# A planner that counts DMA time: order of the first loads, four key projections side by side, and sums of squares on GpSimd

## The chip, the cores and the metric

The kernel runs on one core of one Trainium2 chip. The metric is the device time of one launch in microseconds (us): lower is better. A core has a matrix engine (PE, with its weight loads shown as PEld), a vector engine (DVE), an activation engine (ACT), GpSimd (POOL) and a queue engine that issues the DMAs (SP). Each engine works through its own instructions in the order in which they stand in the program. An instruction that has to wait for a semaphore holds up everything behind it on its engine.

## The reference, cut to what matters

Two transformer-like blocks run one after the other on x of 512 tokens by 2048 features. All arithmetic is 32-bit. The change touches mainly the beginning of the first block:

```python
mem_n = rms_norm(mem, mem_norm_g)               # mem: 256 x 2048
h = rms_norm(x, norm_g[i])                      # x: 512 x 2048
proj = jnp.einsum("bsd,de->bse", h, dn_w_in[j])
kv = jnp.einsum("bmd,de->bme", mem_n, w_kv)     # 1024 columns of k, 1024 of v
k = rms_norm(kv[..., :XA_WIDTH].reshape(B, -1, XA_HEADS, XA_DIM), kn_g)
v = kv[..., XA_WIDTH:].reshape(B, -1, XA_HEADS, XA_DIM)
# ... gated delta rule on proj, cross attention on k and v, gate, w_out,
# then a second block (mLSTM, HGRN2, w_out_2, a gated feed of p)
```

## The kernel before, in words

**Tiling.** Tensors lie with features on the 128 partitions. x is 16 tiles `xraw` of 128x512 (256 KB each), mem is 8 tiles `mraw`, each of which holds two feature tiles of 128x256 (256 KB each). A projection is a `Job`: 128 output columns, accumulated over 16 feature tiles in one PSUM bank. Its weights arrive in four *pieces* `raw` of four feature tiles (256 KB each). To keep 32-bit accuracy, every operand is split into two parts: `hi`, a rounded copy made by ACT, and `lo`, the rest, made by DVE (`lo = raw - hi`). Each feature tile takes three matmuls: hi by hi, hi by lo, lo by hi. So one piece is 12 matmuls, and each piece costs one ACT and one DVE instruction of 128x512 ahead of it.

**The order.** The program's order is written once, when the kernel is built, by the class `Driver`. It keeps a modelled clock for each engine (`clk`, line 87). Every helper (`act`, `tt`, `stt`, `mm`) emits an instruction and moves the clock of its engine (`_on`, line 105). A task (a Python generator) runs on when its own time `tau` is no later than the modelled PE clock; `run` (line 348) picks the task with the lowest priority number that may run, and otherwise the next unit of a projection (`_unit`, line 315). A time that is modelled too early puts an instruction into its engine's queue too early, where it then blocks. `calm` (line 222) holds back background work while the clocks of ACT or DVE are too far ahead of PE's.

**DMAs.** All of them are issued by SP. `_pump` (line 266) loads the pieces, at most six buffers `raw` at a time, and takes for the landing of piece i the later of PE's clock plus 3.0 us and 4.5 + 1.5 i us. `d.dma` (line 171), used for everything that is stored and loaded later on, adds 2.3 us. Neither knows of other transfers under way.

**The beginning.** `first_loads` (line 447) adds one load behind each of the first 24 pieces: `mraw` 1 to 7 behind the first seven, then `ident`, `norm_g` and `xraw` 0, then one `xraw` behind each piece. The key projections 0 and 1 run side by side (their pieces alternate), all others one by one. `mem_task` (line 560) splits mem's tiles, then sums mem's squares; the sum passes through PE (`col_sum`) and ACT, and the result `f_rm` is what every key and value evacuation (`evac_k`, `evac_v`) waits for. `x_task` (line 591) makes the square of each `xraw` on ACT (`xsq`) and adds it to `xsum` on DVE. When the sum is done, sixteen `part` tasks scale each tile (DVE), copy it to `xh` (ACT) and take the rest `xl` (DVE). The first projection of x (`w_xq`) comes behind the last value projection. In `x_task` the load's time `f_x[k].tau` is read by `need`, but nothing yields between that and the emission of `xsq`.

Of the kernel before, what the change touches and what calls it, by code (L numbers as in the profile page):

```python
# [16 lines left out]
MUL, ADD, SUB, MAX = ALU.mult, ALU.add, ALU.subtract, ALU.max  # L17

T = 512
NM = 256  # L20
C = 128
NCH = T // C
# [56 lines left out]
class Driver:  # L79
# [4 lines left out]

    def __init__(self, tc, wp, psp, sp):
        self.tc, self.nc, self.wp, self.psp, self.sp = tc, tc.nc, wp, psp, sp
        self.clk = dict(pe=0.0, act=0.0, dve=0.0, pool=0.0)
        self.tau = 0.0
        self.tasks = []
        self.units = []  # L90
        self.pieces = []
        self.i_unit = self.i_dma = self.i_hi = self.i_spl = self.i_mm = 0
        self.spl_end = []
        self.nbank, self.nacc, self.maxacc = 0, 0, 6
        self.bank_t = [0.0] * 8
        self.bank_of = {}
        self.live = 0
        self._dep, self._last = 0.0, None
        self.held = {}
        self.nslot = 0  # L100
        self.table = None
        self.nhead, self.head = 0, None
# [65 lines left out]
                              is_transpose=True if tr else None)  # L168
        self._on("pe", c, LP)

    def dma(self, out, in_, lat=2.3):
        self.nc.sync.dma_start(out=out, in_=in_)
        self.tau = max(self.tau, self.clk["pe"]) + lat


    def slot(self, shape=(128, T), dt=F32, name="s", reserve=0):
# [89 lines left out]
    def _pump(self):  # L266
        while self.i_dma < len(self.pieces):
            r = self.i_dma - RAW
            if r >= 0 and (r >= self.i_spl or self.spl_end[r][1] > self.clk["pe"]):
                break  # L270
            j, c0, n = self.pieces[self.i_dma]
            raw = self.wp.tile([128, KC, 128], F32, tag="raw", bufs=RAW, name="raw")
            self.nc.sync.dma_start(out=raw[:, :n, :j.w.shape[2]], in_=j.w[:, c0:c0 + n])
            self.pieces[self.i_dma] = (j, c0, n, raw, max(self.clk["pe"] + 3.0, 4.5 + 1.5 * self.i_dma))
            self.i_dma += 1
            if self.i_dma <= self.nhead:
                self.head(self.i_dma)
        while self.i_hi < self.i_dma and self.i_hi < self.i_mm + SPL:
            j, c0, n, raw, tau = self.pieces[self.i_hi]
            if tau > self.clk["pe"] and self.i_hi > self.i_mm:  # L280
                break
            hi = self.wp.tile([128, KC, 128], F32R, tag="hi", bufs=SPL, name="hi")
            self.tau = tau
            m = j.w.shape[2]
            self.act(hi[:, :n, :m], raw[:, :n, :m], AF.Copy)
            self.pieces[self.i_hi] = (j, c0, n, raw, hi, self.tau)
            self.i_hi += 1
        while self.i_spl < self.i_hi:
            j, c0, n, raw, hi, tau = self.pieces[self.i_spl]
            if tau > max(self.clk["pe"], self.clk["dve"]) and self.i_spl > self.i_mm:  # L290
                break
            self.tau = tau
            if j.narrow:
                lo = None
                self.tt(hi[:, :n, 64:], raw[:, :n, :64], hi[:, :n, :64], SUB)
            else:
                lo = self.wp.tile([128, KC, 128], F32R, tag="lo", bufs=SPL, name="lo")
                self.tt(lo[:, :n], raw[:, :n], hi[:, :n], SUB)
            self.pieces[self.i_spl] = (j, c0, n, hi, lo, self.tau)
            self.spl_end.append((self.i_spl, self.tau))  # L300
            self.i_spl += 1
# [94 lines left out]
def build(ctx: ExitStack, tc: tile.TileContext, A, out):  # L396
# [47 lines left out]
    for k in range(KT):  # L444
        xraw.append(d.slot_now(name="xraw"))

    def first_loads(i):

        if i < len(mraw):
            nc.sync.dma_start(out=mraw[i], in_=A["memT"][:, 2 * i:2 * i + 2])  # L450
        elif i < len(mraw) + KT:
            k = i - len(mraw)
            if k == 0:
                nc.sync.dma_start(out=ident, in_=A["ident"])
                nc.sync.dma_start(out=norm_g, in_=A["norm_g"])
            nc.sync.dma_start(out=xraw[k], in_=A["xT"][:, k])
            d.give(f_x[k])
            f_x[k].tau = d.clk["pe"] + 3.0

    f_x = [Fut() for _ in range(KT)]  # L460
    resetb = const.tile([128, T], F32, name="resetb")
    nc.vector.memset(resetb, 1.0)
# [97 lines left out]
    def mem_task():  # L560
        hs = []
        for i, t in enumerate(mraw):
            d.tau = 3.8 + 1.5 * i
            yield
            tau = d.tau
            hi = yield from slot(dt=F32R, name="mh")
            lo = yield from slot(dt=F32R, name="ml")
            hi = hi.rearrange("p (k m) -> p k m", k=2)
            lo = lo.rearrange("p (k m) -> p k m", k=2)
            for j in range(2):  # L570
                g = mem_norm_g[:, 2 * i + j:2 * i + j + 1]
                d.tau = tau
                act(hi[:, j], t[:, j], AF.Copy, scale=g)
                stt(lo[:, j], t[:, j], g, hi[:, j], MUL, SUB)
                give(M.f[2 * i + j], (hi[:, j], lo[:, j]))
        ssum = None
        t0 = d.tau
        for i, t in enumerate(mraw):
            d.tau = t0
            yield from d.calm(AHEAD)  # L580
            t = t.rearrange("p k m -> p (k m)")
            act(t, t, AF.Square)
            if i == 0:
                ssum = t
            else:
                tt(ssum, ssum, t, ADD)
                free(t)
        tt(ssum[:, :NM], ssum[:, :NM], ssum[:, NM:], ADD)
        yield from ones_sum([ssum[:, :NM]], NM, 1.0 / D, f_rm)

    def x_task():
        ssum = yield from slot(name="xsum")
        for k, t in enumerate(xraw):
            yield from need(f_x[k])
            yield from d.calm(AHEAD)
            q = yield from slot(name="xsq")
            act(q, t, AF.Square)
            if k == 0:
                cp(ssum, q)
            else:  # L600
                tt(ssum, ssum, q, ADD)
            free(q)
        f = Fut()
        yield from ones_sum([ssum], T, 1.0 / D, f)
# [134 lines left out]
    def evac_ab(job):  # L739
# [19 lines left out]
               rows[0:32, (n + 1) * C - 1:(n + 1) * C], SUB, -1.0, MUL)  # L759
        dgc = tc.dram_tile([32, T], F32, name="dgc")  # L760
        yield
        d.dma(dgc, rows[0:32])
        pt = yield from transpose4(rows)
        for nm in ("gb", "ngc", "beta", "kdec", "nbeg"):
            gate[nm] = const.tile([128, NCH, 32], F32, name=nm)
# [497 lines left out]
    def evac_if(job):  # L1263
# [33 lines left out]
        dws = tc.dram_tile([32, NCH], F32, name="dws")  # L1297
        yield
        for j, r in enumerate((mu, wi, en)):
            d.dma(drow[j], r[0:32], lat=0)  # L1300
        d.dma(dws, ws[:, 0:NCH])
        t0 = d.tau
        pt = yield from transpose4(rows)
        wc = const.tile([128, NCH, 64], F32, name="wc")
# [2 lines left out]
        wsb = const.tile([128, 32, NCH], F32, name="wsb")  # L1307
        d.tau = t0
        yield
        d.dma(wsb, bc(dws, 0, 128))  # L1310
        free(w, fx, nb, mu, wi, en, rows, sp_)
        mlg.update(drow=drow, wc=wc, wsb=wsb)
        give(f_if)
# [26 lines left out]
    def ml_task(h):  # L1340
# [4 lines left out]
        for j in range(3):  # L1345
            t = yield from slot(name="rowb")
            yield
            d.dma(t, mlg["drow"][j, h:h + 1].broadcast_to((128, T)))
            rr.append(t)
        muR, qd, enR = rr  # L1350
        yield
# [381 lines left out]

    first_loads(0)
    d.head = first_loads
    d.nhead = len(mraw) + KT
    d.spawn(mem_task(), 1)
    d.spawn(x_task(), 2)
    jk = [Job(A["w_k"][e], M, evac_k(e), NM) for e in range(2 * XH)]
    jv = [Job(A["w_v"][e], M, evac_v(e), NM) for e in range(2 * XH)]  # L1740
    d.add(jk[0], jk[1])
    for j in jk[2:] + jv[:-2]:
        d.add(j)
    jv[-1].drop = True
    d.add(jv[-2], jv[-1])
# [241 lines left out]
```

## Time and profile before

| what | us |
|---|---|
| median of 3 runs | 2911.86 (2909.01 to 2912.65) |
| the profiled execution | 2909.73 |
| its span, first to last instruction | 2907.8 |
| PE busy in the span | 2852.8 (98%) |
| DVE busy, ACT busy, POOL busy | 1713.4, 1389.0, 80.7 |
| DMA, mean over the span | 106 GB/s |

The profiled execution lies 2.13 us below the median of the runs. PE is busy for nearly the whole span. What is left to it are its idle gaps, and stretches in which its matmuls are slower than elsewhere. The views by stretch show in which part of the run these lie, and the timeline shows which instruction of which engine each of them ended with.

### The profile page before, as it was taken

To read this page: it belongs to the slowest core of one execution; us is meant where nothing else is said; L and a number is where in the kernel's file an instruction comes from. 1 tells how busy PE (TensorE), PEld (TensorE's weight loads), DVE (VectorE), ACT (ScalarE), POOL (GpSimd) and SP (SyncE) were. 2 spreads that over 40 slices of the span, in tenths; PEclk is the share of its full clock that TensorE was granted. 3 is DMA by queue.
4 is the path that set the end of the run, shared out by engine and by line. 5 is a ranking of instruction groups with operands and counts; after the bars stand their busy time and mean duration, and the time that the engine had idled before them with its cause. 6 is when DMAs were issued, how large, how long until landed. Compare 5 with 4: busy or idle time off the path is not lost. (4 is left out here: it accounts for less than half of the span.)

```text
span 2907.8 us, 40891 instructions
## 1 busy us (share of the span) xinstructions
PE 2852.8 (98%) x14936; PEld 2382.5 (82%) x14936; DVE 1713.4 (59%) x3285; ACT 1389.0 (48%) x2627; POOL 80.7 (3%) x178
## 2 busy tenths in 40 slices
PE   7999999999999999999999999999999999999997
PEld 7877887788788888888888878888888888888886
DVE  6746677778777777635333464455655556444445
ACT  6544645565545555435222334444554556433433
POOL 0000000100000100000000000000000000000000
PEclk9999999999999999999999999999999999999998
DMA  7422422233222332354433433222222222333233
GB/s 244 145 80 93 122 94 88 95 98 98 83 89 98 95 98 91 102 169 127 130 119 119 151 104 109 91 77 80 84 84 77 91 84 88 116 122 110 95 98 109
DMA packets 177865, 308.92 MB, mean 106 GB/s; under 512 B 25216, under 2 KB 32000, under 8 KB 177664
## 3 DMA queue, kind: packets, MB, share of 16 engines
q1 hardware_dynamic: 177664, 306.31, 33.1%
q8 instruction: 117, 1.92, 0.3%
q14 instruction: 84, 0.69, 0.1%
HBM read 290.24 MB, written 15.99 MB: 105 GB/s over the span
## 5 line engine op out<-in xcount | busy, mean ns | idle before, releaser
L131 DVE TENSOR_TENSOR lo<-raw,hi 128x512 fp32r<-128x512 f32 x948 | 638.5, 685 | 624.4 <-ACT hi L120 605.5
L120 ACT ACTIVATE hi<-raw 128x512 fp32r<-128x512 f32 x956 | 586.9, 621 | 868.6 <-PE acc L167 762.4
L167 PE MATMUL acc<-xh,hi 128*128 128x512 f32 x1424 | 582.5, 409 | 0.7 <-ACT xh L120 0.4
L167 PE MATMUL acc<-xl,hi 128*128 128x512 f32 x1424 | 556.2, 391 | 2.8 <-DVE xl L131 2.7
L167 PE MATMUL acc<-xh,lo 128*128 128x512 f32 x1408 | 551.4, 392 | 4.5 <-DVE lo L131 4.4
L167 PE MATMUL acc<-x2h,hi 128*128 128x512 f32 x1040 | 415.8, 400 | 0.0
L167 PE MATMUL acc<-x2l,hi 128*128 128x512 f32 x1040 | 405.2, 390 | 0.0
L167 PE MATMUL acc<-x2h,lo 128*128 128x512 f32 x1024 | 399.8, 390 | 0.0
L167 PEld LDWEIGHTS acc<-xh,lo 128*128 128x128 f32 x1408 | 264.4, 188 | 63.8 <-DVE lo L131 6.2
L167 PEld LDWEIGHTS acc<-xl,hi 128*128 128x128 f32 x1424 | 268.4, 189 | 54.6 <-DVE xl L131 4.0
L167 PEld LDWEIGHTS acc<-xh,hi 128*128 128x128 f32 x1424 | 268.2, 188 | 53.6 <-issue 1.7
L167 PE MATMUL acc<-ph,hi 128*128 128x512 f32 x768 | 298.8, 389 | 0.0
L167 PE MATMUL acc<-pl,hi 128*128 128x512 f32 x768 | 298.8, 389 | 0.0
L167 PE MATMUL acc<-ph,lo 128*128 128x512 f32 x768 | 298.8, 389 | 0.0
L167 PEld LDWEIGHTS acc<-x2h,lo 128*128 128x128 f32 x1024 | 192.2, 188 | 41.5
L167 PEld LDWEIGHTS acc<-x2l,hi 128*128 128x128 f32 x1040 | 195.7, 188 | 37.0
L167 PEld LDWEIGHTS acc<-x2h,hi 128*128 128x128 f32 x1040 | 195.6, 188 | 37.2
L167 PEld LDWEIGHTS acc<-pl,hi 128*128 128x128 f32 x768 | 144.1, 188 | 30.1
L167 PEld LDWEIGHTS acc<-ph,lo 128*128 128x128 f32 x768 | 144.1, 188 | 29.9
L167 PEld LDWEIGHTS acc<-ph,hi 128*128 128x128 f32 x768 | 144.1, 188 | 29.8
L134 DVE SCALAR_TENSOR_TENSOR cv<-acc,c_dn_conv,cv 128x511 f32<-128x511 f32 x144 | 107.3, 747 | 35.6 <-ACT cv L120 32.1
L131 DVE TENSOR_TENSOR Xb<-Xb,Nb 128x16 f32<-128x16 f32 (+30 forms) x372 | 113.7, 306 | 8.8
(321 smaller groups left out, 3631.4 us busy)
## 6 DMA issues: line engine op xcount, KB each, us to landing
raw<-w_qkv SPq DMA_DIRECT2D x192, 256.0 KB, 3.1
raw<-w_out SPq DMA_DIRECT2D x192, 256.0 KB, 2.9
raw<-w_z SPq DMA_DIRECT2D x128, 256.0 KB, 3.2
raw<-w_pg SPq DMA_DIRECT2D x68, 256.0 KB, 3.0
gR<-dgc SPq DMA_DIRECT2D x48, 256.0 KB, 3.9
raw<-w_k SPq DMA_DIRECT2D x32, 256.0 KB, 4.8
raw<-w_v SPq DMA_DIRECT2D x32, 256.0 KB, 3.7
raw<-w_xq SPq DMA_DIRECT2D x32, 256.0 KB, 3.1
```

The costliest lines, as they stand in the source:

```text
L120: self.nc.scalar.activation(out=out, in_=in_, func=func, **kw)
L131: self._v(eng, free_size(out)).tensor_tensor(out=out, in0=a, in1=b, op=op)
L134: self._v(None, free_size(out)).scalar_tensor_tensor(out=out, in0=a, scalar=s, in1=b, op0=op0, op1=op1)
L167: self.nc.tensor.matmul(out, lhsT=lhsT, rhs=rhs, start=start, stop=stop, is_transpose=True if tr else None)
```

## The change

Six things change; the instructions' arithmetic stays what it was.

1. The planner gets a clock for SP (0.5 us for each issue) and a time `dq` up to which the DMA engines are busy. `land` returns when a transfer has landed: issue plus 2.0 us at least, and 0.7 us (1.1 us in the first 9 us) of the engines for every 256 KB.
2. `_pump` and `d.dma` take their times from `land`. With nothing else under way a piece lands at PE's clock plus 3.05 us (3.0 before), and a `d.dma` at plus 3.85 us (2.3 before).
3. The first loads follow a list: `mraw` 0; `mraw` 1 behind piece 0; 2 and 3 behind pieces 2 and 3; 4 and 5 behind pieces 6 and 7; 6 and 7 behind pieces 10 and 11. `xraw` 0 and 1 come behind pieces 4 and 5, 2 and 3 behind 8 and 9, 4 and 5 behind 12 and 13, and `xraw` 6 to 15 behind pieces 15 to 24.
4. `mem_task` waits for each tile's modelled landing instead of a fixed time, and `x_task` yields once between `need` and `xsq`.
5. The sums of x's squares (one copy, 15 adds of 128x512) run on POOL instead of DVE.
6. The key projections 0 to 3 run side by side instead of 0 and 1.

```diff
-        self.clk = dict(pe=0.0, act=0.0, dve=0.0, pool=0.0)
+        self.clk = dict(pe=0.0, act=0.0, dve=0.0, pool=0.0, sp=1.2)
+        self.dq = 0.0
...
-    def dma(self, out, in_, lat=2.3):
+    def land(self, n=128 * T, extra=0.1):
+
+        t = max(self.clk["pe"], self.clk["sp"])
+        self.clk["sp"] = t + 0.5
+        self.dq = max(self.dq, t + 2.0)
+        self.dq += (0.7 if self.dq > 9 else 1.1) * n / (128 * T)
+        return self.dq + 0.25 + extra
+
+    def dma(self, out, in_, extra=0.9, n=128 * T):
         self.nc.sync.dma_start(out=out, in_=in_)
-        self.tau = max(self.tau, self.clk["pe"]) + lat
+        self.tau = max(self.tau, self.land(n, extra))
...
-            self.pieces[self.i_dma] = (j, c0, n, raw, max(self.clk["pe"] + 3.0, 4.5 + 1.5 * self.i_dma))
+            self.pieces[self.i_dma] = (j, c0, n, raw, self.land(n * 128 * j.w.shape[2]))
...
+    loads = [[] for _ in range(1 + 3 * KT)]
+    for i in range(len(mraw)):
+        loads[4 * (i // 2) + (i % 2 if i < 2 else i % 2 - 1)].append(("m", i))
+    n = 0
+    for i in range(len(loads)):
+        if n < KT and (i % 4 in (1, 2) and i > 4 if i < KT else i >= KT):
+            loads[i].append(("x", n))
+            n += 1
+
     def first_loads(i):
 
-        if i < len(mraw):
-            nc.sync.dma_start(out=mraw[i], in_=A["memT"][:, 2 * i:2 * i + 2])
-        elif i < len(mraw) + KT:
-            k = i - len(mraw)
+        for what, k in loads[i] if i < len(loads) else ():
+            if what == "m":
+                nc.sync.dma_start(out=mraw[k], in_=A["memT"][:, 2 * k:2 * k + 2])
+                f_m[k].tau = d.land()
+                f_m[k].done = True
+                continue
             if k == 0:
                 nc.sync.dma_start(out=ident, in_=A["ident"])
                 nc.sync.dma_start(out=norm_g, in_=A["norm_g"])
             nc.sync.dma_start(out=xraw[k], in_=A["xT"][:, k])
-            d.give(f_x[k])
-            f_x[k].tau = d.clk["pe"] + 3.0
-
+            f_x[k].tau = d.land(extra=0.5)
+            f_x[k].done = True
+
...
-            d.tau = 3.8 + 1.5 * i
+            d.tau = 0.0
+            yield from need(f_m[i])
             yield
...
             yield from need(f_x[k])
+            yield
             yield from d.calm(AHEAD)
             q = yield from slot(name="xsq")
             act(q, t, AF.Square)
             if k == 0:
-                cp(ssum, q)
+                cp(ssum, q, eng=pool)
             else:
-                tt(ssum, ssum, q, ADD)
+                tt(ssum, ssum, q, ADD, eng=pool)
             free(q)
...
-            d.dma(drow[j], r[0:32], lat=0)
-        d.dma(dws, ws[:, 0:NCH])
+            d.dma(drow[j], r[0:32], n=32 * T)
+        d.dma(dws, ws[:, 0:NCH], n=32 * NCH)
...
-    d.add(jk[0], jk[1])
-    for j in jk[2:] + jv[:-2]:
+    d.add(*jk[:4])
+    for j in jk[4:] + jv[:-2]:
         d.add(j)
```

What is left out sets the sizes of a few later transfers in the same way, and the count of first loads.

## Rows read from the trace of the kernel before

**Rows 1.** The page: span, and busy time of each engine.

```profile
span 2907.8 us, 40891 instructions
PE 2852.8 (98%) x14936; PEld 2382.5 (82%) x14936; DVE 1713.4 (59%) x3285; ACT 1389.0 (48%) x2627; POOL 80.7 (3%) x178
```

**Rows 2.** Stretches: length, busy (instructions) of each engine, granted clock, DMA share, GB/s.

```profile
0.00:10.00 10.00, 3.57 (x15) 3.27 (x16) 4.11 (x13) 5.05 (x9) 0.20 (x4) 1.00 0.70 203
10.00:20.00 10.00, 6.62 (x49) 6.28 (x48) 5.75 (x13) 5.83 (x13) 0.00 (x0) 1.00 0.97 313
20.00:30.00 10.00, 9.78 (x69) 9.68 (x69) 9.61 (x18) 9.69 (x20) 0.00 (x0) 0.83 0.89 311
30.00:40.00 10.00, 8.12 (x64) 7.54 (x63) 7.03 (x13) 6.57 (x12) 0.00 (x0) 1.00 0.90 269
40.00:50.00 10.00, 7.25 (x59) 6.83 (x57) 6.22 (x15) 7.12 (x17) 0.00 (x0) 1.00 0.68 229
60.00:70.00 10.00, 10.00 (x85) 10.00 (x85) 7.49 (x15) 6.26 (x13) 0.00 (x0) 1.00 0.60 183
120.00:130.00 10.00, 6.84 (x27) 4.47 (x26) 10.00 (x17) 5.24 (x9) 0.00 (x0) 1.00 0.16 53
```

**Rows 3.** Timeline of PE: start, length, tiles; idle before it and its releaser.

```profile
9.53 0.41 PE L167 MATMUL acc<-mh,hi 128*128 128x256 f32 x1
9.74 0.41 PE L167 MATMUL acc<-ml,hi 128*128 128x256 f32 x1
...
19.59 0.39 PE L167 MATMUL acc<-mh,hi 128*128 128x256 f32 x1 [3.38 <-ACT hi L120]
...
36.20 0.39 PE L167 MATMUL acc<-mh,lo 128*128 128x256 f32 x1 [1.80 <-DVE lo L131]
...
50.01 0.39 PE L167 MATMUL acc<-mh,lo 128*128 128x256 f32 x1 [2.71 <-DVE lo L131]
...
115.38 0.40 PE L167 MATMUL acc<-xh,hi 128*128 128x512 f32 x1
...
124.94 0.50 PE L167 MATMUL acc<-xl,hi 128*128 128x512 f32 x1 [1.84 <-DVE xl L131]
```

**Rows 4.** Timeline of ACT: the first square of x, mem's last, one of k's norms.

```profile
18.39 0.63 ACT L120 ACTIVATE xsq<-xraw 128x512 f32<-128x512 f32 x1 [3.68 <-DMA xraw<-xT]
...
21.71 0.90 ACT L120 ACTIVATE mh<-mraw,c_mem_norm_g 128x256 fp32r<-128x256 f32 x2
...
37.06 0.42 ACT L120 ACTIVATE mraw<-mraw 128x256 f32<-128x256 f32 x1
...
90.45 0.62 ACT L120 ACTIVATE xsq<-xraw 128x512 f32<-128x512 f32 x1
```

**Rows 5.** Timeline of DVE: behind k's norm, the first part of x, the last.

```profile
48.47 0.88 DVE L134 SCALAR_TENSOR_TENSOR xk<-xk,c_xa_kg,sq 128x256 f32<-128x256 f32 x2 [1.85 <-ACT sq L120]
...
96.10 0.75 DVE L134 SCALAR_TENSOR_TENSOR xraw<-xraw,norm_g,xsum 128x512 f32<-128x512 f32 x1 [0.18 <-ACT xsum L120]
...
129.14 1.28 DVE L131 TENSOR_TENSOR xl<-xraw,xh 128x512 fp32r<-128x512 f32 x2
```

**Rows 6.** POOL by line and shape: its adds' nearest rows, count, busy, mean ns.

```profile
L149 POOL TENSOR_SCALAR_AFFINE_SELECT gR<-gR 128x512 f32<-128x512 f32 x24 | 16.4, 685 | 552.0 <-DMA gR<-dgc 466.2 <-DVE Xb L881 49.9 <-PE p L167 26.8
L131 POOL TENSOR_TENSOR out<-h1r,gt 128x256 f32<-128x256 f32 x6 | 5.3, 920 | 399.5 <-PE ss L167 399.5
```

**Rows 7.** Timeline of DVE at the end: beside POOL's products, and alone.

```profile
2890.86 2.67 DVE L134 SCALAR_TENSOR_TENSOR out<-h1r,c_fin_w,gt 128x256 f32<-128x256 f32 x3
...
2897.16 1.66 DVE L134 SCALAR_TENSOR_TENSOR out<-h1r,c_fin_w,gt 128x256 f32<-128x256 f32 x4
```

**Rows 8.** Waits of PE from 130 to 2850 us: total, times, longest.

```profile
PE acc L167 <- DVE lo L131: 4.4, 3, 3.2
PE pst L167 <- DVE ud L131: 3.2, 1, 3.2
PE tr L167 <- DVE pr L131: 3.0, 4, 1.3
```

More of the change, by code (lines that the diff above doesn't have):

```diff
@@ L456, in first_loads @@
             nc.sync.dma_start(out=xraw[k], in_=A["xT"][:, k])
-            d.give(f_x[k])
-            f_x[k].tau = d.clk["pe"] + 3.0
+            f_x[k].tau = d.land(extra=0.5)
+            f_x[k].done = True
+    f_m = [Fut() for _ in mraw]
     f_x = [Fut() for _ in range(KT)]
@@ L579, in mem_task @@
             d.tau = t0
+            yield from need(f_m[i])
             yield from d.calm(AHEAD)
@@ L761, in evac_ab @@
         yield
-        d.dma(dgc, rows[0:32])
+        d.dma(dgc, rows[0:32], n=32 * T)
         pt = yield from transpose4(rows)
@@ L1309, in evac_if @@
         yield
-        d.dma(wsb, bc(dws, 0, 128))
+        d.dma(wsb, bc(dws, 0, 128), n=32 * T)
         free(w, fx, nb, mu, wi, en, rows, sp_)
@@ L1347, in ml_task @@
             yield
-            d.dma(t, mlg["drow"][j, h:h + 1].broadcast_to((128, T)))
+            d.dma(t, mlg["drow"][j, h:h + 1].broadcast_to((128, T)), 1.5)
             rr.append(t)
@@ L1735, in build @@
     d.head = first_loads
-    d.nhead = len(mraw) + KT
+    d.nhead = len(loads) - 1
     d.spawn(mem_task(), 1)
```

## The prediction

> **What bounds the kernel now.** Read the page first: PE is busy for 2852.8 of 2907.8 us [rows 1], so at most 55 us of its idle time can be won, and an edit that doesn't touch a PE gap or a slow stretch of matmuls is worth nothing. Then the busy time by stretch [rows 2]. Full flow is the stretch from 60 to 70 us: 85 instructions in 10 us, 0.118 us each (I take 0.12 for a mem matmul of 256 columns). The 50 us before it are poorer. Missing to 10 us are 6.43, 3.38, 0.22, 1.88 and 2.75 us; from 120 to 130 another 3.16, there with DVE busy for all ten. Third, the timeline of PE says what ended each gap [rows 3]: at 19.59 an ACT copy `hi`, at 36.20 and 50.01 a DVE `lo`, at 124.94 a DVE `xl`. These are in-order blocks, not missing work: at 18.39 ACT had stood 3.68 us in front of the first `xsq`, whose x had not landed, with `hi` of the next piece behind it [rows 4]; at 48.47 DVE had stood 1.85 us in front of `xk`, which waits for ACT's norm, with `lo` behind it [rows 5].
>
> The clock adds to this. In the first five busy microseconds matmuls start 0.21 us apart (9.53, 9.74) [rows 3], which is 256 columns at 1.2 GHz, though the clock column prints 1.00 there. After the 3.38 us gap the granted clock of the next stretch is 0.83, and its 69 instructions fill 9.78 us where 69 x 0.118 = 8.1 would do [rows 2]. So that gap was paid twice, with 1.6 us on top.
>
> From 130 us on, PE's waits are a dozen gaps inside the recurrences, 3.2 us the longest; those named add up to 10.6 us [rows 8].
>
> **The change, part by part.**
>
> *Square of x in front of `hi`.* The new yield lets the planner place `xsq` only once `land` says that x has landed. By the model `xraw` 0 is the tenth 256 KB load: 3.2 + 5 x 1.1 us for the first ones, then 0.7 each, so 13.4 us with its margin. The trace moves 7.75 units of 256 KB by 10 us (203 GB/s) and 11.9 per 10 us after that (313 GB/s) [rows 2], so unit 10.25 (`ident` is a quarter) is there at 12.1 us. The block of 3.38 us and the slow 1.6 us behind it go.
>
> *Four keys side by side.* Each mem tile feeds four jobs instead of two, so the first 192 matmuls need 16 pieces and 8 mem tiles, 24 units; the same number of matmuls before needed the same units, but the first 96 needed 16 of them, and now need 8 pieces and 4 mem tiles, 12. PE's first two pieces end at 11.2 us as now (1.2 GHz). From there one piece takes 12 x 0.12 = 1.44 us, so piece i would start at 11.2 + 1.44 (i - 2). Landing by the rate above against that, with 1.3 us for `hi` and `lo` in between (0.63 as `xsq` of that shape, 0.64 as half of `xl`'s 1.28) [rows 4, 5]: piece 8 is unit 17.25, landed at 18.0, needed at 18.5; piece 12 is unit 25.25, 24.7 against 24.3; piece 15 is unit 30.25, 28.9 against 28.6; piece 24 is unit 48.25, 44.0 against 41.6. So there is no stall up to piece 12, and then the pieces come up to 2.4 us late, because from piece 15 every piece has an x behind it: 1.68 us of transfer for 1.44 us of matmuls. After `xraw` 15 nothing but weights is loaded and this ends. New stall: 2.4 us, bounds 0 (349 GB/s, what 311 at a share of 0.89 would be at full share) and 5 (269 GB/s from 30 us on, as in that stretch [rows 2]).
>
> *The norms of mem and k.* All four first jobs end together, at about 32 us, and wait for `f_rm`. Today it is there at 37.5, 15.7 us after mem's last tile was taken up at 21.71 [rows 4]. That tile is now unit 24.25, landed at 23.9; plus 15.7 is 40. The planner lets six sums stand open (`maxacc`), so jobs 4 and 5 hide the wait until piece 24, at 43 to 45 us. If `f_rm` came later than that, PE would wait for the rest, us for us. The gaps of 1.88 and 2.75 us belong to these chains; two heads are evacuated at once now, and DVE has no `xsum` in between. I keep 1.5 us of their 4.63 (bounds 0 and 4.63).
>
> So up to 115.38, the first `xh` matmul [rows 3], the gaps of 3.38 + 0.22 + 1.88 + 2.75 = 8.2 us and the slow 1.6 us (9.8 together) are replaced by 2.4 + 1.5 = 3.9 us: a gain of 5.9 us, bounds 0 and 9.8.
>
> *x's sums on POOL and the stage of x.* No POOL add of 128x512 is in this trace. The nearest rows are a one-input select of that size, 685 ns, and a two-input product of half the size, 920 ns [rows 6], so 0.69 to 1.84 us; I take 1.84, since two inputs count, and the planner charges 1.38. In the plan the squares and sums run one after the other: 0.54 + 0.3 + 1.38 + 0.3 = 2.5 us for each x. `xraw` 6 comes at about 31 us, so the last add ends at 31 + 10 x 2.5 = 56 at the earliest, perhaps 75 with `calm` holding it back. Today the last square is at 90.45 [rows 4], the first `part` at 96.10 and the last `xl` ends at 130.4 [rows 5], 34 us for work that DVE has to fit between `lo`s. With parts from 56 to 75 on they end by 90 to 109, and the first projection of x starts at 115.4 - 5.9 = 109.5. The 3.16 us of 120 to 130 go (bounds 0 and 3.16).
>
> What POOL costs DVE: beside POOL's products three of DVE's take 2.67 us, alone four take 1.66 [rows 7], 0.89 against 0.42 us. At twice the size that is up to 1 us for the one DVE instruction that each of the 16 POOL instructions may hold up. The 16 DVE instructions that go (0.64 us each as half of `xl`'s 1.28 [rows 5], 10 us) cover most of that; without them DVE would have been busy for some 8 of the 10 us from 20 to 30, its fullest stretch of the first 50, where today it is 9.61 [rows 2]. I take 0 on PE, 0 to 16 as bounds, the upper one as a rival below.
> The Trainium skill (SBUF — State Buffer, section "SBUF: two separate sides") states that GpSimd and a DVE instruction with two SBUF inputs lock the shared port pair against each other for a whole instruction. The trace agrees with an alternation of the two (0.89 against 0.42). By the Trainium skill (GPSIMD Engine Reference, section "2.1 Instruction dispatch") a two-input body needs about 2.5 cycles per element, an estimate of 1.07 us for 512 at 1.2 GHz; the last sum would be no earlier by it, since the planner's 2.5 us set the pace.
>
> *Times of all other transfers.* A piece's landing stays at 3.0 to 3.05 us, so the order in steady flow is nearly kept. What is loaded by `d.dma` is used 1.55 us later in the plan. Those loads are made well ahead, and no wait of PE names a DMA [rows 8]. But any shift makes the planner choose other neighbours in the recurrences. I take 0, bounds plus and minus 5 us, about half of the 10.6 us of gaps that can be dealt anew [rows 8].
>
> **Sum.** 5.9 + 3.2 + 0 = 9.1 us off the profiled execution's 2909.73; against the median of the runs, 2911.86, I give 2903. Bounds: 2911.9 - 9.8 - 3.2 - 5 = 2894 and 2911.9 - 0 - 0 + 5 = 2917. A measurement of this kernel can tell about 0.2%, 5.8 us, from no change, so the line is at 2906.
>
> **The rivals.**
>
> *Hidden behind the loads.* The same 50 us must still bring in 13.3 MB, of which 12.9 MB (49.25 units) stand before and with `xraw` 15; from 10 to 40 us the DMA share is 0.89 to 0.97 already [rows 2]. If the rate is 269 GB/s from 30 us on, the loads cost 5 us and pieces trickle in, DVE's waits for norms fall due at the same time (4.6 us), and only the 3.16 us of the x stage are won: 9.8 - 9.6 + 3.2 = 3.4 us, so 2909. For it: the share. Against: for 24 matmuls four keys take three units where two keys took four, and pieces of the first 20 us come early. A fresh deal of the recurrences against me by 4 us ends in the same place. Chance 0.26.
>
> *POOL in front of `lo`, slower.* From 13 to about 60 us pieces come just in time, so every `lo` is on PE's path. If each of POOL's 16 instructions holds up a `lo` by 1 us [rows 7] and PE gets none of it back, that is 16 us against a gain of 9.1: 2919. It decides from 9 of the 16 on to no gain at all, and from 15 to a loss of over 5.8 us. For it: the doubled times at the end. Against: where loads are the bound, a late `lo` delays the piece once, and PE makes it good from the next piece that has landed. Chance 0.07.
> The reason for it would be the lock that the Trainium skill (SBUF — State Buffer, section "SBUF: two separate sides") describes.
>
> *It doesn't do what it says.* The plan runs on 0.107 us for a matmul where the trace has 0.12, and on 0.7 us for a load where it has 0.84; if the two drifted apart, `xsq` would block ACT again. Both lag alike (2.5 us at piece 15 each), so I leave it at 0.02, about 2911, within the second rival's band.
>
> **How the numbers follow.** Forecast 2903, chance 0.65 (2894 to 2906, faster). Hidden behind the loads or no effect: 0.28, 2906 to 2915. POOL: 0.07, slower. The range that leaves out no more than 2 in 10 reaches from 2894 into the second case, to 2911. Faster 0.65, same 0.28, slower 0.07.
>
> **What would show it.** Right: no ACT wait of over 1 us in front of `xsq`; granted clock 1.00 from 20 to 30 us; the first `xh` matmul near 110 us; first `part` between 58 and 80, and PE idle for under 0.5 us behind the first `xh`. Wrong: PE gaps between 24 and 45 us that add up to over 5 us (loads), `lo` of over 1 us beside POOL adds with PE gaps behind them (the lock), a gap ended by `xk` or `f_rm` near 43 us (open sums), or PE idle from 130 to 2850 us that differs by over 5 us from now.

## The result and the profile after

The changed kernel takes 2930.02 us (2929.07 to 2930.98, four runs) against 2911.77 for the kernel before beside it: a ratio of 1.0059, interval 1.0046 to 1.0071. It is slower by some 18 us where 2903 was forecast, outside the range and with the other sign.

The page of the kernel after, against [rows 1]: span, and busy time of each engine.

```profile
span 2927.3 us, 40895 instructions
PE 2862.5 (98%) x14936; PEld 2387.5 (82%) x14936; DVE 1712.2 (58%) x3269; ACT 1394.8 (48%) x2631; POOL 98.1 (3%) x194
```

PE does the same 14936 matmuls, is busy for 9.7 us more and idle for 9.8 us more: there are new gaps, and slower matmuls with them. Five instructions of the timelines tell in which part of the run they lie:

| starts, us | before | after | later by |
|---|---|---|---|
| first matmul of mem (`mh`) | 6.29 | 6.67 | 0.4 |
| first matmul of x (`xh`) [rows 3] | 115.38 | 112.87 | -2.5 |
| first evacuation of a projection of x (`xq<-acc`) | 131.69 | 134.43 | 2.7 |
| first matmul of `w_out` (`ph`) | 1337.85 | 1342.33 | 4.5 |
| first matmul of `w_out_2` (`p_h`) | 2688.97 | 2708.40 | 19.4 |
| end of the span | 2907.8 | 2927.3 | 19.5 |

So the beginning won 2.5 us, the stage of x lost 5.2 against that, the long middle to 1338 lost 1.7, and 15 us were lost behind the first `ph`, more than a thousand microseconds after the beginning, which the change is mainly about. These starts are of one execution each and move by some microseconds. Three of the kernels below (old time, pace of `y_loader` and mask's cast) have the same instructions in the same order as the changed one on ACT and DVE up to 130 us; their first `xh` starts at 111.69, 114.02 and 114.50, their first `xq<-acc` at 133.24, 136.31 and 136.05. So the 2.5 us won in the beginning are anything from 0.9 to 3.7, while the stage from the first `xh` to the first `xq<-acc` lost 5.2 to 6.0 in all four, and the 15 us behind `ph` are not in doubt.

The stretches of after (length, busy time and instructions of PE, PEld, DVE, ACT and POOL, granted clock, DMA share, GB/s) show the same; the first five answer to [rows 2], the last is the place of the loss.

```profile
10.00:20.00 10.00, 9.45 (x75) 9.01 (x74) 5.67 (x12) 7.13 (x15) 2.13 (x2) 1.00 0.96 277
20.00:30.00 10.00, 7.80 (x62) 7.59 (x63) 8.10 (x14) 8.55 (x17) 2.59 (x2) 1.00 1.02 374
...
50.00:60.00 10.00, 7.82 (x46) 7.02 (x45) 7.66 (x18) 7.75 (x19) 0.00 (x0) 0.83 0.33 101
110.00:120.00 10.00, 6.72 (x43) 5.63 (x41) 9.35 (x17) 6.32 (x12) 0.00 (x0) 0.97 0.48 155
120.00:130.00 10.00, 8.13 (x22) 6.10 (x23) 9.56 (x16) 4.50 (x8) 0.00 (x0) 0.68 0.08 26
1330.00:1380.00 50.00, 36.06 (x142) 26.72 (x141) 30.45 (x55) 26.58 (x49) 0.00 (x0) 0.90 0.43 139
```

The same fifty microseconds of the kernel before, in the same columns, are full:

```profile
1330.00:1380.00 50.00, 50.00 (x222) 41.40 (x221) 24.93 (x46) 22.04 (x39) 0.00 (x0) 1.00 0.44 136
```

PE's waits of after from 130 to 2870 us (what PE waited for: total, times, longest) name what stands in the way; [rows 8] has no such line.

```profile
PE acc L168 <- DVE pl L132: 12.4, 8, 10.6
...
PE acc L168 <- ACT ph L121: 1.5, 1, 1.5
```

No wait in the whole list names a DMA, here as little as in the kernel before. What PE waits for has passed through ACT or DVE, and the late transfer stands one step further back.

`pl` and `ph` are the two parts of `y`, the result of the gate, which is read back from DRAM (`yscr`) tile by tile as the operand of `w_out`. The timeline of PE in after shows the gap, and matmuls half as fast behind it (0.43 us apart where they were 0.23 ahead of it):

```profile
1342.33 0.50 PE L168 MATMUL acc<-ph,hi 128*128 128x512 f32 x1 [1.50 <-ACT ph L121]
1343.26 0.49 PE L168 MATMUL acc<-pl,hi 128*128 128x512 f32 x1 [0.43 <-DVE pl L132]
...
1355.55 0.80 PE L168 MATMUL acc<-pl,hi 128*128 128x512 f32 x1 [10.62 <-DVE pl L132]
1356.14 0.63 PE L168 MATMUL acc<-ph,lo 128*128 128x512 f32 x1
1356.57 0.63 PE L168 MATMUL acc<-ph,hi 128*128 128x512 f32 x1
```

DVE, which makes `pl`, was not busy: it stood for 8.99 us in front of another instruction (timeline of DVE, after):

```profile
1342.52 1.28 DVE L132 TENSOR_TENSOR pl<-y,ph 128x512 fp32r<-128x512 f32 x2
1352.80 0.63 DVE L1480 CAST lmask<-lm 128x512 uint8<-128x512 f32 x2 [8.99 <-DMA lm<-lmask]
...
1354.81 2.49 DVE L132 TENSOR_TENSOR pl<-y,ph 128x512 fp32r<-128x512 f32 x4
```

In the kernel before, the same cast stands for 2.10 us. The mask that DVE waits for here was late because SP issued it behind a burst of `y` loads. SP's queue in after (start, time in which its issues lie, tile):

```profile
1331.53 0.42 SPq L181 DMA_DIRECT2D y<-yscr  x1
1333.87 3.05 SPq L282 DMA_DIRECT2D raw<-w_out  x2
1337.01 0.38 SPq L181 DMA_DIRECT2D y<-yscr  x1
1339.31 3.04 SPq L282 DMA_DIRECT2D raw<-w_out  x2
1342.45 3.71 SPq L181 DMA_DIRECT2D y<-yscr  x8
1346.20 0.48 SPq L181 DMA_DIRECT2D xr<-xT  x1
1346.73 1.50 SPq L1479 DMA_DIRECT2D lm<-lmask  x2
```

In the kernel before, one `y` went behind every piece, and the last was out by 1306.95:

```profile
1304.27 0.38 SPq L172 DMA_DIRECT2D y<-yscr  x1
1306.57 0.33 SPq L273 DMA_DIRECT2D raw<-w_z  x1
1306.95 0.43 SPq L172 DMA_DIRECT2D y<-yscr  x1
```

The pitch is 5.44 us after, 2.72 before. One piece is 12 matmuls of 0.227 us, 2.72 us. The task `y_loader` is a loop: load a tile, move its own time `tau` by what `d.dma` adds, load the next. With 2.3 us its time has passed when one piece is done; with 3.85 it has not, and it runs again one piece later. That 1.55 us more of planner time costs 2.72 us for each tile is the theory that the experiments test first. Its rivals: POOL's sums, or the mask alone.

### The profile page after: what moved, and what is told of

It is laid out like the page before. It is cut to its first block, busy times and chain, and to the rows that moved or that the text cites. A ratio compares the mean times of both kernels' runs of the same rounds, so it can differ in the third digit from the quotient of the medians.

```text
span 2927.3 us, 40895 instructions
## 1 busy us (share of the span) xinstructions
PE 2862.5 (98%) x14936; PEld 2387.5 (82%) x14936; DVE 1712.2 (58%) x3269; ACT 1394.8 (48%) x2631; POOL 98.1 (3%) x194
## 5 line engine op out<-in xcount | busy, mean ns | idle before, releaser
L168 PE MATMUL acc<-pl,hi 128*128 128x512 f32 x768 | 300.4, 391 | 12.4 <-DVE pl L132 12.4
```

The costliest lines, as they stand in the source:

```text
L168: self.nc.tensor.matmul(out, lhsT=lhsT, rhs=rhs, start=start, stop=stop, is_transpose=True if tr else None)
```

## Experiments on the loss behind w_out

Each time below stands beside one of the kernel before from the same rounds (medians of 2912.72 to 2914.06 us, 2911.77 beside the changed kernel), and each ratio is against that. As those medians move by some 2 us, a difference of that size between kernels of different rounds says nothing.

**The old time of `d.dma` back in the changed kernel.** The rest of the change stays, and `land` still counts the transfer.

```diff
-        self.tau = max(self.tau, self.land(n, extra))
+        self.land(n, extra)
+        self.tau = max(self.tau, self.clk["pe"]) + 2.3
```

> The changed kernel, with the time that the planner adds after a transfer of d.dma back at 2.3 us; the DMA clock goes on running, so pieces and first loads keep theirs. Theory A, the longer time (3.85 us and more) paces the loader of the y tiles, one in 5.44 us instead of one in 2.72, and w_out starts before its operands: the loads stand 2.72 us apart again, PE's waits for pl (12.4 us) fall under 1 us, the median is 2913 to 2917 against 2930. Theory B, the loss sits in the first 135 us and in the new order of the recurrences: the median stays within 3 us of 2930.

Measured: 2912.01 us, ratio 1.000 (0.9991 to 1.0010), 18.0 us less than the changed kernel. `y` goes out every 2.72 us, and PE has no wait at all from 1290 to 1400 us. So the whole loss hangs on the time that `d.dma` adds.

**That number alone, in the kernel before.**

```diff
-    def dma(self, out, in_, lat=2.3):
+    def dma(self, out, in_, lat=3.85):
```

> The kernel before, with one number changed: d.dma adds 3.85 us instead of 2.3. Theory A says that this alone brings the loss: y tiles 5 us or more apart instead of 2.72, PE waits for ph and pl of 10 us or more at the start of w_out, a median 10 to 16 us over before. If the DMA clock (which lets a load count more when weights were issued just ahead of it) is needed for it, the tiles stay under 4.5 us apart and the loss under 6 us.

Measured: 2930.71 us, ratio 1.0055 (1.0040 to 1.0070), 16.7 us more than before. Nothing of the DMA clock, the list, POOL or the keys is in it, and it makes the same picture. Its SP queue ends in a burst and the mask stands behind it; its PE waits from 1290 to 1420 us name the same two tiles, with 10.2 us for 12.4:

```profile
1344.01 2.81 SPq L172 DMA_DIRECT2D y<-yscr  x6
1347.38 1.00 SPq L1455 DMA_DIRECT2D lm<-lmask  x2
```

```profile
PE acc L167 <- DVE pl L131: 10.2, 8, 8.3
PE acc L167 <- ACT ph L120: 1.5, 1, 1.5
```

**The pace of `y_loader` alone put back.** All other loads keep their new times.

```diff
+            t0 = max(d.tau, d.clk["pe"])
             d.dma(t, yscr[i])
             give((f_yl if i < 2 * XH else f_yf)[i], t)
+            d.tau = t0 + 2.3
```

> The changed kernel, with one line more in the loader of the y tiles: what is loaded still counts as landed by the DMA clock, but the loader itself goes on 2.3 us after each issue. Theory A (the pace of this one loader): the same as with the old time everywhere, 2913 to 2917, y loads 2.72 us apart, no wait for pl over 1 us. If the longer time does its damage in other places too, the median lies at 2920 or above although pl is no longer waited for.

Measured: 2912.07 us, ratio 0.9998 (0.9989 to 1.0008). So of all the loads whose times were changed it is this one loop that costs; PE's waits for `pl` are 0.5 us in all. Together the three kernels settle the cause.

**The mask's cast later.** The two casts are placed 12 us of planner time behind their loads, and `y_loader` keeps its slow pace. (Not shown: the task that calls this code now yields there, and the load of `lb` moves ahead of the casts.)

```diff
-            nc.sync.dma_start(out=t[:, :i1 - i0], in_=A["lmask"][:, i0:i1])
-            nc.vector.tensor_copy(out=lmask[:, i0:i1], in_=t[:, :i1 - i0])
-            free(t)
+            d.dma(t[:, :i1 - i0], A["lmask"][:, i0:i1])
+            raws.append((i0, i1, t))
...
+        d.tau = d.clk["pe"] + 12.0
+        yield
+        for i0, i1, t in raws:
+            nc.vector.tensor_copy(out=lmask[:, i0:i1], in_=t[:, :i1 - i0])
+            free(t)
```

> The changed kernel, with the casts of the level masks placed 12 us (planner's time) behind the issue of their loads, so that DVE doesn't stand in front of them (8.99 us). y is loaded as slowly as before. Theory E, the 10.62 us gap of PE is this one in-order wait of DVE: the gap goes, what is left of PE's waits for pl is under 4 us, the median is 2918 to 2922. Theory F, the tiles are late because the loads are late and the masks only stand beside that: PE waits about as long, in more and shorter gaps, 2926 to 2930.

Measured: 2921.01 us, ratio 1.0026 (1.0015 to 1.0037): 9.0 us less than the changed kernel, 9 more than with the pace mended. The waits of this kernel from 1290 to 1420 us are those for `y` alone:

```profile
PE acc L168 <- DVE pl L132: 3.9, 8, 2.1
PE acc L168 <- ACT ph L121: 1.5, 1, 1.5
```

So the slow pace costs twice: about half because the operands come late, half because the burst pushes a mask that nobody needs yet behind it, and the mask's cast stands in DVE's queue in front of the operands. From the first `ph` to the first `p_h` the changed kernel takes 1366.1 us, this one 1357.7, the one with the pace mended 1352.0 (before: 1351.1); so 8.4 us there are the cast's and 5.7 the late operands'.

## Experiments on the beginning and on POOL

With the pace mended the change is worth nothing (2912.07 beside 2913.25), though a gain of 9.1 us had been forecast. The first `xh` lies at 114.02 in that kernel, and the first `part` at 106.52, where the forecast had 58 to 80. The trace of after shows why the sum is late. ACT's squares and POOL's adds (timelines, after):

```profile
40.74 0.61 ACT L121 ACTIVATE xsq<-xraw 128x512 f32<-128x512 f32 x1
62.59 0.62 ACT L121 ACTIVATE xsq<-xraw 128x512 f32<-128x512 f32 x1
...
97.03 0.62 ACT L121 ACTIVATE xsq<-xraw 128x512 f32<-128x512 f32 x1
```

```profile
22.05 1.29 POOL L132 TENSOR_TENSOR xsum<-xsum,xsq 128x512 f32<-128x512 f32 x1 [3.01 <-ACT xsq L121]
...
97.79 1.30 POOL L132 TENSOR_TENSOR xsum<-xsum,xsq 128x512 f32<-128x512 f32 x1 [1.83 <-ACT xsq L121]
```

SP issues the last tile of x at 38.22 us, and its tiles take 7.1 us at most to land. Yet no square is made from 41 to 62 us, and then the eleven that are left come 3.44 us apart on average ((97.03 - 62.59) / 10), with POOL idle for more than half of it. Three theories: `calm` holds the squares back while four heads are evacuated together; POOL's modelled add sets their pace; POOL's adds keep DVE off their shared port.

**Sums on DVE in the changed kernel.**

```diff
-                cp(ssum, q, eng=pool)
+                cp(ssum, q)
...
-                tt(ssum, ssum, q, ADD, eng=pool)
+                tt(ssum, ssum, q, ADD)
```

> The changed kernel, with the sums of x's squares on DVE again. Theory C, the chain from square to POOL sum to the next square paces x_task (3.1 us for one x from 63 us on) and makes x's parts late: the first part starts before 100 us instead of 105.4, PE's waits for xl (4.0 us) halve, the median is 2 to 5 us under 2930. Theory D, it is calm that holds x_task back (41 to 63 us without a square): the first part stays within 3 us of 105, no gain. If POOL's port lock slowed DVE, the lo beside its adds (1.17 us where 0.69 is usual) go back to 0.69.

Measured: 2924.23 us, ratio 1.0043 (1.0028 to 1.0058), 5.8 us less than the changed kernel. The last square is at 89.06 and the first `part` at 95.43. That is some 6 us for POOL, not the 18 of the whole; the two ratios' intervals still overlap, and the next pair decides.

**The same with `y_loader`'s pace mended.** (The edit of the last kernel, and the three lines in `y_loader`.)

> The changed kernel with both mends: the y loader paced as before (2930 to 2912) and the sums of x's squares on DVE (2930 to 2924). If the two losses add up, 2906, that is 6 us under before: the gain that was forecast for the first 135 us, without what took it back. If the order of the recurrences changes more than these, 2909 to 2913.

Measured: 2906.03 us, ratio 0.9972 (0.9962 to 0.9982): again 6.0 us less than with POOL (2912.07; ratio 0.9998, 0.9989 to 1.0008), now with intervals apart. The two causes add up.

**POOL keeps the sums, but the squares don't wait for it in the plan.** The pace of `y_loader` is mended. The adds still run one behind the other; only the task's own time goes back to the end of the square.

```diff
             act(q, t, AF.Square)
+            t0 = d.tau
             if k == 0:
                 cp(ssum, q, eng=pool)
             else:
                 tt(ssum, ssum, q, ADD, eng=pool)
             free(q)
+            tp, d.tau = d.tau, t0
+        d.tau = max(d.tau, tp)
```

> The changed kernel with the y loader paced as before, the sums on POOL, but x_task goes on when the square is done instead of when POOL's add is done. Theory C (the chain through POOL sets the pace): squares under 2.5 us apart once they run, first part before 100 us, median 2 to 5 us under 2912. Theory H (POOL's lock on DVE's port is what costs): same pace and same 2912, lo of over 1 us beside the adds.

Measured: 2903.26 us, ratio 0.9964 (0.9952 to 0.9977), 8.8 us less than with the same sums paced. The first `part` moves from 106.52 to 87.55. So it was not POOL's work that cost these microseconds, but the place where the plan put the squares because of it. In this kernel they stand close together (ACT's timeline):

```profile
63.20 0.62 ACT L121 ACTIVATE xsq<-xraw 128x512 f32<-128x512 f32 x1
64.64 1.14 ACT L121 ACTIVATE xsq<-xraw 128x512 f32<-128x512 f32 x2
```

The adds stand as close, and a `lo` beside them takes twice its time (POOL and DVE, timelines). But PE waits for no `lo` from 60 us on:

```profile
62.52 6.16 POOL L132 TENSOR_TENSOR xsum<-xsum,xsq 128x512 f32<-128x512 f32 x4 [20.18 <-ACT xsq L121]
```

```profile
64.76 1.31 DVE L132 TENSOR_TENSOR lo<-raw,hi 128x512 fp32r<-128x512 f32 x1 [0.40 <-ACT hi L121]
```

**A looser hold, with the sums on DVE.**

```diff
             yield from need(f_x[k])
             yield
-            yield from d.calm(AHEAD)
+            yield from d.calm(6.0)
```

(`AHEAD` is 1.5 us; the pace of `y_loader` is mended, too.)

> As the last, and x_task's squares may be placed while ACT's or DVE's clock is 6.0 us ahead of PE's instead of 1.5. Theory D, calm holds x_task back from 44 to 62 us: the squares come without that gap, the last before 80 us, the first part before 85, PE's waits for xl go (3.1 us with the sums on DVE): 2 to 4 us under the last. Theory G, the squares are held back because ACT and DVE have no time for them: they push lo and hi aside, PE's gaps between 40 and 65 us grow by as much as the x stage gains.

Measured: 2901.34 us (2900.12 to 2901.80), ratio 0.9954 (0.9939 to 0.9968): the lowest median here, below the kernels before and after. The kernels of 2902.21 and 2903.26 us can't be told from it. Squares now go on to 47.61 us and again from 61.69, the first `part` is at 84.85, PE waits for no `xl`, and from 110 to 130 us it is busy throughout.

**The looser hold, with the sums on POOL.** (The squares not held by POOL's time, `calm(6.0)`, and the pace of `y_loader` mended.)

> The kernel with the y loads at their old pace and POOL's adds off the squares' pace (2903.26 us) gets the looser hold (6.0 us) of the squares as well. Theory 'the hold keeps the squares back while four keys are evacuated': with both loosened the last square is done by 80 us, the first part by 86, no xl wait; the kernel with the sums on DVE had 2901.34 us with this hold, so the same place gives 2900 to 2902. Rival 'POOL locks DVE's port while the pieces come just in time': the squares of 41 to 62 us now bring POOL adds among the last lo's and the evacuations, PE gaps on DVE lo up to 62 us grow by up to 1 us for each add, and the time is 2903 to 2908. Third: the x stage was already free of waits at 2903.26, so nothing moves (2902 to 2904).

Measured: 2910.05 us, ratio 0.9989 (0.9979 to 0.9998). Only the engine of the sums and the planner's time for them tell it from the kernel of 2901.34, and it is 8.7 us slower. The first `xh` lies at 120.28 instead of 113.92, and the first evacuation of x's projections at 132.2 instead of 125.9; those 6.3 us lie in the beginning, and the rest behind it. Here the adds run while the pieces are still coming in. POOL, DVE and PE in this kernel (timelines):

```profile
30.50 1.83 POOL L132 TENSOR_TENSOR xsum<-xsum,xsq 128x512 f32<-128x512 f32 x1 [0.58 <-ACT xsq L121]
```

```profile
30.48 4.09 DVE L132 TENSOR_TENSOR lo<-raw,hi 128x512 fp32r<-128x512 f32 x3
...
36.81 5.12 DVE L132 TENSOR_TENSOR lo<-raw,hi 128x512 fp32r<-128x512 f32 x3
...
43.25 0.68 DVE L132 TENSOR_TENSOR lo<-raw,hi 128x512 fp32r<-128x512 f32 x1
```

```profile
38.61 0.58 PE L168 MATMUL acc<-mh,lo 128*128 128x256 f32 x1 [2.30 <-DVE lo L132]
```

Two groups of three `lo` take 4.09 and 5.12 us, 1.4 and 1.7 for each, beside POOL's adds, and one alone 0.68; the add in the first row takes 1.83 us instead of 1.29. PE waits 2.30 us behind them; up to 135 us its waits for `lo` are 7.2 us here and 1.5 us in the kernel of 2901.34. The mechanism of the prediction's second rival is real. The tight `calm` of the changed kernel happens to keep most adds out of the stretch in which pieces come just in time.
The Trainium skill (SBUF — State Buffer, section "SBUF: two separate sides") says that the shared port pair is locked for the whole instruction and not split, and these rows fit that, with both engines slower side by side. They can't tell a lock from a split by themselves.

**Two keys instead of four, in the fastest kernel.**

```diff
-    d.add(*jk[:4])
-    for j in jk[4:] + jv[:-2]:
+    d.add(*jk[:2])
+    for j in jk[2:] + jv[:-2]:
```

> The fastest kernel so far (2901.34 us: y loads at the old pace, sums on DVE, looser hold) with two key projections side by side instead of four. Theory 'four keys side by side feed PE from fewer loads': with two, the first 96 matmuls need 16 units of 256 KB instead of 12, so the PE gaps on hi or mh between 10 and 30 us grow by 2 to 4 us, while the evacuations come two heads at a time and their gaps (0.5 to 2.5 us) move; the time is 2903 to 2906. Rival 'the order of the loads did it, not the four keys': with mem's tiles spread behind the pieces, jobs 0 and 1 wait for mem's tiles just as before and nothing is lost or won, 2900 to 2902.5. Third: the list was made for four keys, so that with two keys mem's tiles 6 and 7 come late (behind pieces 10 and 11, where piece 6 and 7 would need them), and PE loses up to 6 us: 2906 to 2908.

Measured: 2906.93 us, ratio 0.9979 (0.9969 to 0.9988), 5.6 us more. By itself this fits the first theory and the third: PE's longest new gap is ended by a tile of mem, and the list was made for four keys.

```profile
17.75 0.38 PE L168 MATMUL acc<-mh,hi 128*128 128x256 f32 x1 [2.48 <-ACT mh L121]
```

**Two keys with the list of the kernel before.**

```diff
     for i in range(len(mraw)):
-        loads[4 * (i // 2) + (i % 2 if i < 2 else i % 2 - 1)].append(("m", i))
+        loads[i].append(("m", i))
...
+    for n in range(KT):
+        loads[len(mraw) + n].append(("x", n))
```

> The fastest kernel (2901.34 us) with two key projections side by side and the list of first loads of the kernel before (mem's tiles 1 to 7 behind the first seven pieces, x's tiles behind the next sixteen), the squares still placed by the modelled landing. Theory 'four keys side by side need fewer loads for the same matmuls': with two and mem early, pieces come late instead, the PE gaps of 10 to 30 us add up to 3 to 7 us on hi or lo, the first xh matmul lies at 117 to 119 us (113.92 with four keys), and the time is 2904 to 2908. Rival 'the 5.6 us that two keys cost with the new list were mem's tiles that this list brings too late for two keys': with mem early they come back, the first xh matmul lies at 113 to 115.5 us and the time is 2900 to 2903.

Measured: 2902.21 us (2900.12 to 2905.37), ratio 0.9963 (0.9949 to 0.9977), against 0.9954 (0.9939 to 0.9968) with four keys and the new list. The rival holds, by the trace more than by the time. The two intervals with two keys overlap a little (0.9969 to 0.9988 with the new list), but the first `xh` is at 111.61 instead of 117.76, even ahead of the rival's range, and the first evacuation of x's projections at 125.95 instead of 129.74. So most of the 5.6 us were the list's, and new list and four keys together are worth nothing that these runs can tell. PE's gap of 3.38 us [rows 3] is gone without either; the two stretches of this kernel where it was, and its slow matmuls, read (columns as above):

```profile
10.00:20.00 10.00, 9.68 (x74) 9.28 (x72) 8.04 (x17) 9.12 (x19) 0.00 (x0) 1.00 0.94 312
20.00:30.00 10.00, 9.03 (x72) 8.73 (x72) 7.34 (x13) 6.56 (x12) 0.00 (x0) 1.00 1.04 376
```

**The yield in front of the square, alone, in the kernel before.**

```diff
             yield from need(f_x[k])
+            yield
             yield from d.calm(AHEAD)
```

> The kernel before with one line of the change alone: the yield between the wait for x's landing and its square. Theory 'the block of 3.38 us and the slow matmuls behind it were the price of a square put into ACT's queue too early': the ACT wait of 3.68 us in front of the first square goes, PE's gap of 3.38 us on hi shrinks to under 1 us and the time falls by 2 to 5 us (2907 to 2910). Rival 'the loads were late anyway': the gap stays, now ended by a DMA of a piece or of mem's tile, within 1 us of the kernel before (2911 to 2913).

Measured: 2913.65 us, ratio 1.0004 (0.9994 to 1.0013). The first theory falls. ACT still stands 3.71 us in front of the first square and PE 3.38 us behind it:

```profile
18.69 0.63 ACT L120 ACTIVATE xsq<-xraw 128x512 f32<-128x512 f32 x1 [3.71 <-DMA xraw<-xT]
```

The time that the square now waits for, PE's clock plus 3.0 us, is still too early: ACT is there 3.71 us before the tile. With the DMA clock, in the kernel of 2902.21 us, the same list of loads has no such wait. So the yield is not enough without a time that is right. That the right time would do nothing without the yield follows from the code, in which nothing lets another task run between the reading of the time and the square; it was not run.

## Why the prediction was wrong

**The step that failed: times of all other transfers.** It read "Those loads are made well ahead, and no wait of PE names a DMA", and took 0 with bounds of 5 us. The waits of before can't show this. A wait of PE never names these loads, as after shows, where they cost it 12.4 us under the name of `pl`; and a load that is made ahead has no wait, and what holds it ahead is the rate at which it is issued. 1.55 us was read as a shift of each use. In a loop whose next load waits for the last one's time it is a pitch, rounded up to whole pieces: 5.44 for 2.72 us. SP's queue in the trace of before, which the prediction doesn't read, shows it: one `y` behind each piece, with 0.4 us to spare (2.72 - 2.3). One number cost 16.7 us alone, and 18 us in the changed kernel. The prediction's own sign of being wrong, PE's idle time from 130 to 2850 us off by over 5 us, is the one that came: 17.5 us before, and 27.6 after (130 to 2870).

**Square of x in front of `hi`: right.** No square waits over 1 us, the 3.38 us gap is gone and the clock from 20 to 30 us is 1.00. The last two experiments say which part did it: the modelled landing time together with the yield, and not the yield alone.

**Four keys, loads: right in size, by luck.** 2.4 us were forecast, and PE's gaps are 2.05 + 0.70. PE's timeline of after, with the gaps of the head and of the stage of x:

```profile
21.50 0.39 PE L168 MATMUL acc<-mh,lo 128*128 128x256 f32 x1 [2.05 <-DVE lo L132]
...
28.21 0.39 PE L168 MATMUL acc<-mh,lo 128*128 128x256 f32 x1 [0.70 <-DVE lo L132]
...
51.45 0.38 PE L168 MATMUL ss<-qh,ones_r 128*128 128x256 f32 x1 [0.32 <-ACT qh L121]
...
54.00 0.38 PE L168 MATMUL ss<-qh,ones_r 128*128 128x256 f32 x1 [1.71 <-ACT qh L121]
...
117.39 0.49 PE L168 MATMUL acc<-xh,hi 128*128 128x512 f32 x1 [1.16 <-ACT xh L121]
...
120.31 0.80 PE L168 MATMUL acc<-xl,hi 128*128 128x512 f32 x1 [2.42 <-DVE xl L132]
```

The larger one comes at 21.5, earlier than piece 15, for which it was forecast, and stands behind a tile of mem, not of x. That the sizes agree is luck. That fewer loads per matmul are worth something at all is not borne out: with two keys and the old list the time is the same.

**Norms of mem and k: mis-sized.** 1.5 us were kept; the gaps of 51.45 and 54.00 us with a third of 0.54 at 45.13 are 2.57 us. The granted clock of the stretch from 50 to 60 is 0.83 besides, where 46 instructions fill 7.82 us; at 0.118 us each they would take 5.4, so some 2.4 us more. That is 5.0 for 1.5, so 3.5 us more, and about what the head fell short by: 2.5 us won instead of 5.9. With starts that move by up to 3 us between executions the two can't be matched more closely.

**x's sums and the stage of x: wrong by 8.4 us.** A gain of 3.2 was forecast, and a loss of 5.2 came. The term that failed is "the last add ends at 56 at the earliest, perhaps 75": it ended at 99.1. The pace of 2.5 us was 3.44, and the hold by `calm` had no price. Lifting the pace alone moved the first `part` by 19 us and the time by 8.8; lifting the hold, with the sums on DVE, moved them by 10.3 and 4.7.

**POOL's add and the shared port.** 1.30 us was measured, inside the bounds of 0.69 to 1.84, of which the upper was taken. That the lock costs PE nothing nearly held in the changed kernel: beside adds one `lo` took 1.17 us and two `ml` 1.16 for 0.88, and the longest gap of PE behind them is 0.70 us. The rival's price of up to 16 us was about 6.3 in the beginning, and 8.7 in all, once the adds ran among the pieces. The forecast's reason, that PE makes a late `lo` good from the next piece, doesn't hold there.

**The sum.** By spans, 9.1 us were to be won and 19.5 were lost. The 28.6 us between are 3.4 in the head, 8.4 in the stage of x, 16.7 in the middle and behind the first `ph`, and 0.1 at the end. The second rival, POOL, gave a time on the right side for a reason that isn't the main one. With the pace of `y_loader` mended, 2903.26 us are reached by lifting the pace of the squares, and 2901.34 by a looser hold with the sums on DVE; all three mends with the sums on POOL came to 2910.05. So as many microseconds as the forecast counted were there to be won, but by the placing of the squares, and only where POOL's adds keep away from the pieces that come just in time.

**Open.** The time from the first evacuation of x's projections to the first `ph` differs by up to 9.5 us between these kernels (1202.4 with the pace of `y_loader` mended, 1210.1 with the yield alone and 1211.9 with 3.85 us alone in the kernel before). The order in the recurrences is dealt anew by each edit; that this is the reason is likely and not shown. What an edit brought in the beginning and what was added later can be told apart by the starts above, to within 3 us. The looser hold by itself, in the kernel before, was not run, so how much of the 10 us of the fastest kernel needs the DMA clock is open, too.

## What to carry to other kernels

When a planner's or a semaphore's delay is changed, look for loops that pass through it once per item, and cost the pitch, rounded up to the next point at which the loop may run, times the number of items, and not the delay once. A stream that is on time without waits is one whose rate you have to read off its queue, because no list of waits will name it. A start in a single trace carries an error of its own; two kernels with the same beginning show how large it is. Before moving work to an idle engine, ask where the plan will put the work that feeds it, and which instructions of the engine that shares its port will run beside it.

## What the runs showed of the hardware

- POOL's add of two 128x512 operands takes 1.30 us (mean of 15) in the changed kernel, and 1.83 us in the kernel of 2910.05 us, beside DVE's `lo`. The Trainium skill (GPSIMD Engine Reference, section "2.1 Instruction dispatch") states 2.5 cycles per element as the floor of a two-input body, an estimate of 1.07 us; the rows say a fifth more than this estimate.
- A gap costs again through the clock. Behind 10.62 us of waiting the matmuls of 512 columns ran 0.43 us apart, at 1.2 GHz, where they had been 0.23 apart, and the granted clock of the fifty microseconds around is 0.90. From 120 to 130 us of after, behind a gap of 2.42 us that ends at 120.31, it is 0.68.
- The DMA engines brought 374 GB/s from 20 to 30 us at a share of 1.02, where 349 had been worked out for a full share from [rows 2].
